# Turning the SSD results on VectorE in 32x32 blocks, with four block-placing transfers per chunk, and the norm weight moved to the feature split

## The chip, the cores and the metric

One core of a Trainium2 chip runs the whole program. The metric is device time in microseconds (us) of one execution. The engines are TensorE (PE, with its weight loads as PEld), VectorE (DVE), ScalarE (ACT), GpSimd (POOL) and SyncE (SP, which here issues most transfers).

## The reference, cut to what matters

A two-layer network over 1024 latent tokens and 256 context tokens, width 1024. Layer 0 is windowed attention; layer 1 is a bidirectional Mamba-2 SSD mixer with 32 heads of 64 in 8 groups, so 256 features in a group, scanned in chunks of 128 tokens. Its last step, `back`, is what the change touches:

```
def back(y_f, y_b, xs, z):
    n = xs.shape[1]
    y = y_f + y_b + d_skip.astype(f32).reshape(SSD_GROUPS, SSD_HEADS_PER_GROUP, 1) * xs
    u = y.reshape(bsz, n, SSD_WIDTH) * jax.nn.silu(z.astype(f32))
    u = rms_normalize(u.reshape(bsz, n, SSD_GROUPS, SSD_WIDTH // SSD_GROUPS))
    return (u.reshape(bsz, n, SSD_WIDTH) * norm_w) @ w_out
```

The norm is taken per token over the 256 features of a group. `norm_w` has one number for each of the 2048 features, and `@ w_out` sums over the features, so TensorE needs the features on partitions for it.

## The kernel before, in words

All float32 products are made of two rounded halves, "high" (fp32r) and "low" (the rest), with three matmuls each (high·high, high·low, low·high). Layer 0 takes the first 800 us or so; the change lies in layer 1, in `ssd` and `ssd_out`.

`ssd` runs 8 groups of 8 chunks: 64 calls of `slot`, one for each chunk of each group. A slot makes, for 128 tokens (partitions) and 256 features (columns):

- `pcb` (L1281), `po` (L1283, L1284) and, but for a group's last chunk, the state update `S` (L1290) on PE, into banks of the PSUM ring psX (three buffers);
- the decay matrix: `load_rows` (L1260) has SP bring the rows `fd` and `bd` from DRAM two chunks ahead, `offset` (L1264) on POOL adds a column to `bd`, `decays` merges them on DVE (L1269) and takes four exponentials on ACT (L1271); L1285 on DVE multiplies by `pcb`;
- the output: eight PE passes (L1310, `yd`, in psX), added to the POOL sum on DVE (L1319), multiplied by the gate (L1320), squared and summed on ACT (L1322), raised to -1/2 on POOL (L1323), and scaled on ACT (L1328). The result stands in one of two buffers `y`.

While a slot runs, `fill` hands PE the projections of the next group (`front`: L1142, L1151, L1176, with transposes L1084, and DVE work L1037, L1045, L1064), or in the last group the output projection (`ssd_out`, L1570). So there are always matmuls to put between the steps of a slot.

The result of a slot has tokens on partitions. Its `tail` is called in the next slot, after that one's L1310. It turns the 128x256 block with two PE transposes (L1340) into a fourth tenant of psX, ACT evicts each half and multiplies it by the norm weight (L1341; after the turn a feature is a partition, so the weight is a column), and SP writes `uT` to the DRAM tensor `uN` in one transfer (L1342), in rows of 128 tokens, 512 bytes.

In `ssd_out`, SP fetches the features back, 128 features by 512 tokens at a time (L1516, `oraw`), and `split` makes their halves: ACT copies the high half (L1528), DVE subtracts it for the low half (L1525). 32 such pieces feed L1570.

Within the program order that the code gives, a scheduler decides from its own cost estimates where each instruction stands on its engine, and inserts the waits. Each engine runs its own list strictly in that order. SP's list matters too: a transfer that waits for its data holds up all transfers behind it. SP's transfers take their completion semaphores from a ring of eight, so one may also wait for the landing of the eighth before it.

Of the kernel before, what the change touches and what calls it, by code (L numbers as in the profile page):

```python
# [9 lines left out]
F32 = mybir.dt.float32  # L10
BF16 = mybir.dt.bfloat16
F32R = mybir.dt.float32r
AF = mybir.ActivationFunctionType
ALU = mybir.AluOpType
# [3 lines left out]
P = 128  # L18
# [85 lines left out]
class Kernel:  # L104
# [13 lines left out]
    def t(self, pool, shape, dt, tag, bufs=None):  # L118
        self.n += 1
        kw = {"bufs": bufs or BUFS.get(tag, 1)}  # L120
        return pool.tile(shape, dt, tag=tag, name=f"{tag}_{self.n}", **kw)
# [1070 lines left out]
    def ssd(self, c0):  # L1192
        nc, t, a = self.nc, self.t, self.a
        ps = self.psA
# [4 lines left out]
        p = self.ps_ = self.pool("sfront", ctx=c0)  # L1199
# [75 lines left out]
        def slot(n, st, M, fill, tick, last):  # L1275

            g, c = divmod(n, NCH)
            cs = slice(c * P, (c + 1) * P)
            xc = X(st, c).rearrange("p (r h) -> p r h", r=R)
            pcb = t(ps, [P, 512], F32, "psX")[:, :P]  # L1280
            nc.tensor.matmul(pcb, st["bT"][:, cs], st["cT"][:, cs], start=True, stop=True)  # L1281
            po = t(ps, [P, 512], F32, "psX")
            nc.tensor.matmul(po[:, :256], st["cT"][:, cs], flat(st["hf"]), start=True, stop=True)  # L1283
            nc.tensor.matmul(po[:, 256:], st["cT"][:, cs], flat(st["hb"][c]), start=True, stop=True)  # L1284
            nc.vector.tensor_tensor(M, M, pcb.unsqueeze(1).broadcast_to([P, R, P]), op=ALU.mult)  # L1285
            if c < NCH - 1:
                S = t(ps, [P, 512], F32, "psX")
                hn = t(ps2, [P, R, HP], F32, "hf")
                decay(hn, st["hf"], g, c, 0)
                nc.tensor.matmul(S[:, :256], B(st, c), flat(st["xw"]), start=True, stop=True)  # L1290
                nc.vector.tensor_add(hn, hn, S[:, :256].rearrange("p (r h) -> p r h", r=R))
                st["hf"] = hn
            y2 = t(ps2, [P, 2, R, HP], F32, "y2")
            nc.vector.tensor_tensor(y2, po.rearrange("p (d r h) -> p d r h", d=2, r=R),
                                    self.eacs[:, c, :].rearrange("p (d q) -> p d q", d=2)[:, :, 4 * g : 4 * g + 4].unsqueeze(3).broadcast_to([P, 2, R, HP]), op=ALU.mult)
            fill(0)
            xs = t(ps2, [P, R, HP], F32, "xs")
            dg = t(ps2, [P, 1], F32, "dg")
            nc.vector.tensor_tensor_reduce(out=flat(xs)[:, :P], in0=pcb, in1=self.ident, scale=1.0, scalar=0.0, op0=ALU.mult, op1=ALU.add, accum_out=dg)
            sk = t(ps2, [P, R], F32, "sk")  # L1300
            nc.vector.scalar_tensor_tensor(sk, in0=self.dtb[:, c, 4 * g : 4 * g + 4], scalar=dg, in1=self.dsk[:, 4 * g : 4 * g + 4], op0=ALU.mult, op1=ALU.add)
            y = ys[n % 2]
            yf = y[:, :256]
            yv = yf.rearrange("p (r h) -> p r h", r=R)
            nc.gpsimd.tensor_tensor(xs, xc, sk.unsqueeze(2).broadcast_to([P, R, HP]), op=ALU.mult)
            nc.gpsimd.tensor_tensor(yv, y2[:, 0], y2[:, 1], op=ALU.add)
            yadd = nc.gpsimd.tensor_tensor(yv, yv, xs, op=ALU.add)
            yd = t(ps, [P, 512], F32, "psX")
            for r in range(R):
                nc.tensor.matmul(yd[:, r * HP : (r + 1) * HP], M[:, r], X(st, c)[:, r * HP : (r + 1) * HP], start=True, stop=True)  # L1310
            if self.tail is not None:
                self.tail(t(ps, [P, 512], F32, "psX"))
            fill(1)
            load_rows(n + 2, 0)
            nM = None
            if n + 1 < G * NCH:
                with self.tc.issue_after(yadd.ins):
                    offset(n + 1)
            nc.vector.tensor_add(yv, yv, yd[:, :256].rearrange("p (r h) -> p r h", r=R))  # L1319
            ymul = nc.vector.tensor_mul(yf, yf, st["sz"][c])  # L1320
            ss = t(ps2, [P, 1], F32, "ss", 2)
            nc.scalar.activation(y2.rearrange("p d r h -> p (d r h)")[:, :257], y[:, :257], AF.Square, scale=1.0 / 16.0, accum_out=ss)  # L1322
            nc.gpsimd.tensor_tensor(ss, ss, self.half, op=ALU.pow)  # L1323
            fill(2)
            if n + 1 < G * NCH:
                with self.tc.issue_after(ymul.ins):
                    nM = decays(n + 1)
            nc.scalar.activation(yf, yf, AF.Copy, scale=ss)  # L1328
            if c < NCH - 2:
                st["xw"] = xweight(st, g, c + 1, 0)  # L1330
            tick()
            fill(3)
            tick()
            fill(4)
            tick()

            def tail(pt):
                uT = t(ps2, [P, 2, P], F32, "uT")
                for e in range(2):
                    nc.tensor.transpose(pt[:, e * P : (e + 1) * P], yf[:, e * P : (e + 1) * P], self.ident)  # L1340
                    nc.scalar.activation(uT[:, e], pt[:, e * P : (e + 1) * P], AF.Copy, scale=self.nw[:, 2 * g + e : 2 * g + e + 1])  # L1341
                nc.sync.dma_start(self.uN_d[g][:, :, cs].rearrange("e p n -> p e n"), uT)  # L1342

            self.tail = tail
            return nM
# [42 lines left out]
        with ExitStack():  # L1388
            for g in range(G):
                nst = {}  # L1390
                if g < G - 1:
                    work, total = self.front(g + 1, nst, post, st.get("next")), FRONT
                else:
                    cf.close()
                    post.flush()
                    work, total = self.ssd_out(self.pool("out", ctx=c0, side="right"), [(p, [P, 2, 512], F32, "xn4")] * 4, p, ps2, post), OUT * 0.85
                spent = 0.0
                chain = None

                def run(until):  # L1400
                    nonlocal spent
                    while spent < until:
                        cost = next(work, None)
                        if cost is None:
                            return
                        spent += cost
                        post.run(cost)

                def tick():
                    nonlocal chain  # L1410
                    if g < G - 1 and 1 in nst:
                        chain = chain or states(g + 1, nst)
                        next(chain, None)

                for c in range(NCH):
                    def fill(x):
                        run(total * (c + sum(SEGS[: x + 1]) / sum(SEGS)) / NCH)
                    M = slot(g * NCH + c, st, M, fill, tick, g == G - 1)
                if g < G - 1:
                    run(1e9)  # L1420
                    while 1 not in nst or not nst["sz"]:
                        post.pop()
                    chain = chain or states(g + 1, nst)
                    for _ in chain:
                        pass
                    nst["xw"] = xweight(nst, g + 1, 0, 0)
                    st = nst
            self.tail(t(ps, [P, 512], F32, "psX"))
        for _ in work:
            pass  # L1430

    def ssd_out(self, p, spare, sp, sc, post):
# [39 lines left out]
        def tail(s, n, h, r, k, m0):  # L1472
            for m in range(m0, m0 + k):
                if m % 2:
                    nc.gpsimd.tensor_tensor(h[m], h[m], r, op=ALU.mult)
                    nc.scalar.activation(h[m], h[m], AF.Copy, scale=fw[:, m : m + 1])
                else:
                    nc.vector.scalar_tensor_tensor(h[m], in0=h[m], scalar=fw[:, m : m + 1], in1=r, op0=ALU.mult, op1=ALU.mult)
            src = h[m0] if k == 1 else pair[m0][:, :, s - 512 : s - 512 + n]
            dst = a["out"][m0 * P : (m0 + k) * P, s : s + n]  # L1480
            nc.sync.dma_start(dst if k == 1 else dst.rearrange("(a p) n -> p a n", p=P), src)
# [36 lines left out]
        def split():  # L1518
            n = put[0]
            if n < len(feats):  # L1520
                put[0] += 1
                hi, lo = dst[order[n]]

                def low():
                    nc.vector.tensor_sub(lo, feats[n], hi)  # L1525
                    ready.add(order[n])

                post.extend([lambda: nc.scalar.copy(hi, feats[n]), low])  # L1528

        self.oH, self.oL = [None] * 2, [None] * 2  # L1530
        for e in range(2):
# [217 lines left out]
```

## Time and profile before

| | |
|---|---|
| three timed runs | 1806.45, 1807.05, 1812.54 us (median 1807.05) |
| profiled execution | 1804.25 us |
| its span, first to last instruction | 1802.2 us |
| SSD chunks, from the first to the last PE transpose of `tail` | 872 to 1694 us of the span |
| PE busy in that stretch | 817.17 of 822 us |
| DVE, ACT, POOL busy in it | 562.29, 362.94, 409.11 us |
| granted clock of TensorE | 0.994 mean, 1.00 in that stretch |

A profile row such as `L1340 PE MATMUL psX<-ident,y 128*128 128x128 f32 x128 | 35.1, 274 | 0.0` names the line, the engine, the operation, the output and inputs by the program's names, shapes and count; then busy microseconds in all, mean nanoseconds of one, and the idle time of the engine just before these instructions. A timeline row starts with the start and the duration in us. PE instructions overlap: one may start before the one ahead of it has ended, so what a matmul takes of PE's time is the distance from start to start, not its duration.

### The profile page before, as it was taken

The page shows a single profiled execution, that of the slowest core. Times are in us where ns is not written, and L with a number is a line of the kernel's source. Part 1 is how long each engine was busy: PE and PEld are TensorE (multiplying, and loading weights), DVE is VectorE, ACT ScalarE, POOL GpSimd, SP SyncE. Part 2 cuts the span into 40 slices and gives each one's busy share as a digit, 9 for nine tenths or more (in the row PEclk, how much of TensorE's full clock was granted, in tenths as well). Part 3 has the DMA queues.
Part 4 walks back from the last instruction along what each step waited for, and adds up shares of the span by engine and source line. Part 5 has one row for each costly group of instructions (what it writes and reads, how often), then busy time and mean ns, then how long its engine had stood idle before and what let it go on. Part 6 is the DMA issues. An engine that isn't in the chain of part 4 may idle for free.

```text
span 1802.2 us, 28825 instructions
## 1 busy us (share of the span) xinstructions
PE 1741.2 (97%) x10243; PEld 1488.7 (83%) x10243; DVE 1162.7 (65%) x2110; ACT 875.4 (49%) x1897; POOL 815.5 (45%) x1070
## 2 busy tenths in 40 slices
PE   6999998999999899999999999999999999999997
PEld 4797767788898787778898898989889898988886
DVE  3564537787777766675766848667584866765743
ACT  3522235777788666352443534434352443544532
POOL 2441127654466465303454554645455464554422
PEclk9999999999999999999999999999999999999998
DMA  8758865543345445311322323233232333555533
GB/s 300 288 155 256 264 187 149 126 112 96 97 127 131 115 135 196 108 40 51 86 73 79 94 61 92 80 77 82 76 96 62 92 78 80 175 153 174 188 101 123
DMA packets 209391, 227.87 MB, mean 126 GB/s; under 512 B 16096, under 2 KB 149088, under 8 KB 208224
## 3 DMA queue, kind: packets, MB, share of 16 engines
q1 hardware_dynamic: 175184, 207.38, 37.7%
q0 software_dynamic: 34064, 18.65, 5.7%
q8 instruction: 81, 1.33, 0.3%
q14 instruction: 62, 0.51, 0.1%
HBM read 191.14 MB, written 35.13 MB: 126 GB/s over the span
## 4 chain that ended last, share of the span: by engine, by line
PE 85%; DVE 6%; ACT 4%; DMA 3%; issue 2%; SPq 0%; POOL 0%; DVEq 0%; ACTq 0%; POOLq 0%
PE pj L1151 17%; PE pj L1176 10%; PE pj L1570 7%; PE pj L222 7%; PE pj L224 6%; PE pj L223 6%; PE psD L1142 3%; PE pt L693 3%; PE psX L1310 2%; PE pv L700 2%; PE psD L1235 2%; PE pv L699 2%; PE S L668 2%; PE psX L1284 1%; PE psX L1283 1%
## 5 line engine op out<-in xcount | busy, mean ns | idle before, releaser
L222 PE MATMUL pj<-uH,wh 128*128 128x512 f32 (+1 forms) x604 | 223.2, 370 | 6.7 <-DVE rope_b L531 2.3
L224 PE MATMUL pj<-uH,wl 128*128 128x512 f32 (+1 forms) x604 | 211.3, 350 | 0.0
L223 PE MATMUL pj<-uL,wh 128*128 128x512 f32 (+1 forms) x604 | 210.3, 348 | 0.0
L210 POOL TENSOR_TENSOR wl<-wr,wh 128x512 fp32r<-128x512 f32 x92 | 121.7, 1326 | 97.8 <-ACT wh L208 96.6
L1151 PE MATMUL pj<-uH,wh 128*128 128x512 f32 x480 | 161.2, 410 | 2.0 <-ACT xn L1087 1.2
L1151 PE MATMUL pj<-uH,wl 128*128 128x512 f32 x480 | 158.5, 403 | 0.0
L1151 PE MATMUL pj<-uL,wh 128*128 128x512 f32 x480 | 157.2, 401 | 0.0
L698 DVE TENSOR_TENSOR pl<-pt,ph 128x512 fp32r<-128x512 f32 x168 | 114.3, 688 | 60.9 <-ACT ph L697 60.1
L1176 PE MATMUL pj<-wh,uH 128*128 128x256 f32 x512 | 148.0, 289 | 3.1 <-ACT xn L1087 3.0
L1176 PE MATMUL pj<-wl,uH 128*128 128x256 f32 x512 | 150.7, 294 | 0.0
L1212 POOL TENSOR_TENSOR xw<-xn,dtdec 128x256 f32<-128x256 f32 x144 | 93.2, 651 | 127.0 <-PE psD L1235 108.6
L1176 PE MATMUL pj<-wh,uL 128*128 128x256 f32 x512 | 149.5, 292 | 0.0
L222 PEld LDWEIGHTS pj<-uH,wh 128*128 128x128 f32 x604 | 114.2, 189 | 35.2 <-issue 7.8
L1341 ACT ACTIVATE uT<-psX,nw 128x128 f32<-128x128 f32 x128 | 46.9, 366 | 192.9 <-PE psX L1340 192.7
L672 DVE CUSTOM_DVE_ANT_0 sm<-S,mask,nsink 128x640 f32<-128x640 f32 (+2 forms) x160 | 118.8, 773 | 23.2 <-PE S L669 11.5
L208 ACT CAST wh<-wr 128x512 fp32r<-128x512 f32 (+1 forms) x132 | 84.9, 646 | 92.9 <-PE pj L223 73.2
L224 PEld LDWEIGHTS pj<-uH,wl 128*128 128x128 f32 x604 | 114.0, 189 | 17.2 <-issue 1.9
L697 ACT CAST ph<-pt 128x512 fp32r<-128x512 f32 x168 | 97.6, 586 | 62.1 <-PE pt L693 56.3
L223 PEld LDWEIGHTS pj<-uL,wh 128*128 128x128 f32 x604 | 114.5, 190 | 13.1 <-issue 2.5
L674 ACT ACTIVATE sm<-sm,nm 128x640 f32<-128x640 f32 (+2 forms) x160 | 118.6, 742 | 12.2 <-DVE nm L672 11.9
L1151 PEld LDWEIGHTS pj<-uL,wh 128*128 128x128 f32 x480 | 90.1, 188 | 18.9
L1151 PEld LDWEIGHTS pj<-uH,wh 128*128 128x128 f32 x480 | 89.1, 188 | 19.6 <-ACT bn L1087 2.0
(390 smaller groups left out, 5004.6 us busy)
## 6 DMA issues: line engine op xcount, KB each, us to landing
fd<-acs SPq DMA_DIRECT2D x64, 256.0 KB, 5.0
bd<-acs SPq DMA_DIRECT2D x64, 256.0 KB, 5.3
wr<-w_x SPq DMA_DIRECT2D x31, 512.0 KB, 4.0
wr<-w_sk SPq DMA_DIRECT2D x24, 512.0 KB, 4.2
wr<-wg SPq DMA_DIRECT2D x44, 256.0 KB, 4.7
qs<-q POOLq DMA_DIRECT2D x40, 256.0 KB, 3.8
wr<-wo SPq DMA_DIRECT2D x40, 256.0 KB, 2.6
wada<-w_ad SPq DMA_DIRECT2D x8, 1024.0 KB, 6.5
```

Source lines behind the costliest of these rows:

```text
L210: (eng or nc.vector).tensor_tensor(l, raw, h, op=ALU.subtract)
L222: self.nc.tensor.matmul(ps, lh, rh, start=first and i == 0, stop=False)
L223: self.nc.tensor.matmul(ps, lh, rl, start=False, stop=False)
L224: self.nc.tensor.matmul(ps, ll, rh, start=False, stop=last and i == n - 1)
L672: nc.vector.tensor_tensor_reduce(out=sm[:, :W], in0=Sv, in1=self.mask[:, m0 : m0 + W], scale=-SCALE, scalar=self.nsink[:, 4 * j + r : 4 * ...
L674: nc.scalar.activation(sm[:, :W], sm[:, :W], AF.Exp, bias=nm[:, r : r + 1], scale=-1.0, accum_out=sums[:, r : r + 1])
L697: nc.scalar.copy(ph, ptf)
L698: nc.vector.tensor_sub(pl, ptf, ph)
L1151: nc.tensor.matmul(raw[:, 512 * i : 512 * i + 512], l[:, k, :], r[i][:, k, :], start=k + y == 0, stop=k == KT - 1 and y == 2)
L1176: nc.tensor.matmul(pj[:, c], l, r[:, k, :], start=c % 2 + q + k + y == 0, stop=c % 2 == 1 and q == 1 and k == 3 and y == 2)
L1212: nc.gpsimd.tensor_tensor(xw, X(st, c).rearrange("p (r h) -> p r h", r=R), self.dtdec[:, c, hd(d, g)].unsqueeze(2).broadcast_to([P, R, HP] ...
L1570: nc.tensor.matmul(banks[x], l[:, z, sl], r, start=k == 2 * qs[0] and y == 0, stop=k == 2 * qs[-1] + 1 and y == 2)
```

## The change

The tail no longer uses PE, ACT and PSUM. One VectorE instruction turns the 128x256 block in 32x32 squares: token 32b+j, feature 32f+i goes to partition 32b+i, column 32f+j. Each band of 32 partitions then holds 32 tokens of all 256 features, and one transfer for each band puts its blocks where they belong in `uN`: 256 pieces of 32 tokens, 128 bytes each. So a chunk takes four transfers in place of one, and 1024 pieces in place of 256. Since a feature is no longer alone on a partition in `uT`, the norm weight is left out there; `split` applies it, as a column scale in the ACT copy and in the DVE subtraction.

```
-                self.tail(t(ps, [P, 512], F32, "psX"))
+                self.tail()
...
-            def tail(pt):
-                uT = t(ps2, [P, 2, P], F32, "uT")
-                for e in range(2):
-                    nc.tensor.transpose(pt[:, e * P : (e + 1) * P], yf[:, e * P : (e + 1) * P], self.ident)
-                    nc.scalar.activation(uT[:, e], pt[:, e * P : (e + 1) * P], AF.Copy, scale=self.nw[:, 2 * g + e : 2 * g + e + 1])
-                nc.sync.dma_start(self.uN_d[g][:, :, cs].rearrange("e p n -> p e n"), uT)
+            def tail():
+                uT = t(ps2, [P, 256], F32, "uT")
+                nc.vector.transpose(uT, yf)
+                for b in range(4):
+                    dst = self.uN_d[g].rearrange("e (b p) n -> p (e b) n", p=32)[:, :, c * P + 32 * b : c * P + 32 * b + 32]
+                    nc.sync.dma_start(dst, uT[32 * b : 32 * b + 32].rearrange("p (f n) -> p f n", n=32))
...
                 hi, lo = dst[order[n]]
+                nw = self.nw[:, order[n][1] : order[n][1] + 1]
 
                 def low():
-                    nc.vector.tensor_sub(lo, feats[n], hi)
+                    nc.vector.scalar_tensor_tensor(lo, in0=feats[n], scalar=nw, in1=hi, op0=ALU.mult, op1=ALU.subtract)
                     ready.add(order[n])
 
-                post.extend([lambda: nc.scalar.copy(hi, feats[n]), low])
+                post.extend([lambda: nc.scalar.activation(hi, feats[n], AF.Copy, scale=nw), low])
```

The scheduler places the changed program anew from the first tail on. Both places below are from the fourth chunk of the sixth group and the chunk after it. The first is PE's list before: from one chunk's L1310 to the next chunk's `po` and state update (psX_15442 is the ring buffer that the transposes fill; cacc, cctx, pj and psD belong to the projections).

```order
L1310 MATMUL psX_15437<-xn_3030_13955,fd_15206 128x64
L1084 MATMUL psD_15220<-ident_63,cctx_15262 128x128 x2
L1310 MATMUL psX_15437<-xn_3030_13955,fd_15206 128x64 x3
L1340 MATMUL psX_15442<-ident_63,y_2198_9138 128x128
L1281 MATMUL psX_15532<-cT_14508,bT_14012 128x128
...
L1340 MATMUL psX_15442<-ident_63,y_2198_9138 128x128
...
L1283 MATMUL psX_15534<-hf_15411,cT_14508 128x256
L1284 MATMUL psX_15534<-hb_3188_14866,cT_14508 128x256
L1290 MATMUL psX_15538<-xw_15505,bn_3034_13959 128x256
```

PE's list in the changed program at the same place.

```order
L1310 MATMUL psX_15395<-xn_2999_13924,fd_15165 128x64 x4
L1281 MATMUL psX_15489<-cT_14472,bT_13980 128x128
L1283 MATMUL psX_15491<-hf_15369,cT_14472 128x256
L1284 MATMUL psX_15491<-hb_3150_14828,cT_14472 128x256
L1084 MATMUL pj_3253_15413<-ident_63,cacc_15414 128x128 x2
...
L1290 MATMUL psX_15495<-xw_15462,bn_3003_13928 128x256
...
L1310 MATMUL psX_15516<-xn_3000_13925,fd_15305 128x64 x4
```

The two transposes are gone, and with psX no longer shared by the tail, the next chunk's `pcb` and `po` stand directly behind L1310. Left out in the changed list, between this L1310 and the next, are 24 matmuls of L1142, 5 of L1151 and 6 transposes of L1084.

The second place is VectorE's list before, from this chunk's L1285 to the next chunk's.

```order
L1285 TENSOR_TENSOR fd_15206<-fd_15206,psX_15404 128x512
L1299 ISA xs_15429,dg_15430<-psX_15404,ident_63 128x128
...
L1294 TENSOR_TENSOR y_3288_15415<-psX_15406,eacs_8749 128x512
L1291 TENSOR_TENSOR hf_15411<-hf_15411,psX_15410 128x256
L1319 TENSOR_TENSOR y_2199_9140<-y_2199_9140,psX_15437 128x256
L1320 TENSOR_TENSOR y_2199_9140<-y_2199_9140,sz_14840 128x256
L1269 COPY_PREDICATED fd_15347<-before_8755,bd_15240 128x512
L1285 TENSOR_TENSOR fd_15347<-fd_15347,psX_15532 128x512
```

VectorE's list in the changed program at the same place.

```order
L1285 TENSOR_TENSOR fd_15165<-fd_15165,psX_15362 128x512
L1299 ISA xs_15387,dg_15388<-psX_15362,ident_63 128x128
...
L1339 STREAM_TRANSPOSE uT_15400<-y_2198_9138 128x256
L1045 SCALAR_TENSOR_TENSOR cacc_15414<-pj_3253_15413,cacc_15414 128x1024
...
L1319 TENSOR_TENSOR y_2199_9140<-y_2199_9140,psX_15395 128x256
L1320 TENSOR_TENSOR y_2199_9140<-y_2199_9140,sz_14802 128x256
L1269 COPY_PREDICATED fd_15305<-before_8755,bd_15199 128x512
L1294 TENSOR_TENSOR y_3265_15500<-psX_15491,eacs_8749 128x512
L1285 TENSOR_TENSOR fd_15305<-fd_15305,psX_15489 128x512
```

The turn L1339 (of the chunk before) stands behind L1285 and L1299, ahead of projection work and of this chunk's L1319; L1294 has moved from ahead of L1319 to behind L1269. On SP's list the four `uN` transfers stand in a row where one stood, and the next chunk's row load `fd` behind them.

More of the change, by code (lines that the diff above doesn't have):

```diff
@@ L1427, in ssd @@
                     st = nst
-            self.tail(t(ps, [P, 512], F32, "psX"))
+            self.tail()
         for _ in work:
```

## The prediction

> **What bounds the kernel now.** I read the page first, then the busy time by stage, then what PE waited for in the stage of the change. The page says that PE is the fullest engine.
>
> ```profile
> PE 1741.2 (97%) x10243; PEld 1488.7 (83%) x10243; DVE 1162.7 (65%) x2110; ACT 875.4 (49%) x1897; POOL 815.5 (45%) x1070
> ```
>
> An average says little about one stage, so here are the busy times of the stretch that holds all chunks, and of what follows (columns: stretch, length, busy us and instructions of PE, PEld, DVE, ACT, POOL, granted clock, DMA share, GB/s).
>
> ```profile
> 872.00:1694.00 822.00, 817.17 (x4948) 725.38 (x4947) 562.29 (x956) 362.94 (x831) 409.11 (x556) 1.00 0.36 99
> ...
> 1694.00:1802.00 108.00, 98.92 (x485) 82.48 (x483) 50.90 (x54) 40.63 (x61) 29.93 (x19) 0.96 0.37 118
> ```
>
> PE is busy for all but 4.8 us of the 822. Its waits there (total us, times, longest) are small, and none is for the tail's work.
>
> ```profile
> PE pj L1176 <- ACT xn L1087: 2.1, 6, 0.3
> PE pj L1084 <- ACT xn L1087: 1.6, 6, 0.3
> PE pj L1570 <- DVE sz L1187: 0.2, 1, 0.2
> ```
>
> So the chunks are bound by how many passes PE is given, not by the chunk's own chain: what is taken from PE's list comes off the end, and work put on VectorE is free until it makes PE wait. Both have to be priced.
>
> **The change part by part.** *The PE transposes go.* Their busy row is not their price, since passes overlap. The price is the distance of starts, in a timeline of PE around one of them.
>
> ```profile
> 897.98 0.61 PE L1151 MATMUL pj<-uH,wh 128*128 128x512 f32 x2
> 898.43 0.39 PE L1151 MATMUL pj<-uL,wh 128*128 128x512 f32 x1
> 898.66 0.27 PE L1340 MATMUL psX<-ident,y 128*128 128x128 f32 x1
> 898.69 0.48 PE L1151 MATMUL pj<-uL,wh 128*128 128x512 f32 x1
> 899.01 0.63 PE L1151 MATMUL pj<-uH,wl 128*128 128x512 f32 x2
> 899.48 0.62 PE L1151 MATMUL pj<-uH,wh 128*128 128x512 f32 x2
> ```
>
> Two 512-column passes take 0.45 to 0.47 us from start to start. From 898.43 to 899.01, 0.58 us, there are two of them and one transpose, which so costs 0.11 to 0.13 us; I take 0.11. All groups of the tail, before:
>
> ```profile
> L1341 ACT ACTIVATE uT<-psX,nw 128x128 f32<-128x128 f32 x128 | 46.9, 366 | 192.9 <-PE psX L1340 192.7
> ...
> L1340 PE MATMUL psX<-ident,y 128*128 128x128 f32 x128 | 35.1, 274 | 0.0
> ```
>
> 128 x 0.11 = 14.1 us leave PE. ACT loses 46.9 us, which is worth nothing by itself: ACT was busy for 363 of 822 us.
>
> The Trainium skill prices a PE transpose higher ("TensorE: Matmul & The Clock Gate", Part 4: PE-mode transpose): about 275 ns for 128x128 in one kernel's context. The trace agrees with that as a duration, 274 ns, and not as what the pass costs among others, 0.11 us.
>
> *The turn comes to VectorE.* No row shows it. The nearest is the shuffle across partitions, on 512 columns; the rows of L1294 (512 columns) and L1319 (256) in the table below say what half the columns do to a duration.
>
> ```profile
> L531 DVE STREAM_SHUFFLE rope_b<-pj 128x512 f32<-128x512 f32 x20 | 14.8, 739 | 0.0
> ```
>
> 739 x 417 / 687 = 0.45 us, my value. From below it is bounded by an add of that size, 0.42, and from above by the longest VectorE row in these chunks, 1.31 (L1064). 64 x 0.45 = 29 us, so VectorE goes from 562 to 591 us, 72% of the stretch: cover on average, but not everywhere. The new order packs the chunks more tightly. The costliest VectorE groups from 1100 to 1560 us (columns as on the page):
>
> ```profile
> L1064 DVE TENSOR_TENSOR wl<-wr,wh 128x1024 fp32r<-128x1024 f32 x26 | 34.0, 1306 | 15.4 <-ACT wh L1060 15.4
> L1269 DVE COPY_PREDICATED fd<-before,bd 128x512 f32<-128x512 int32 x36 | 32.0, 889 | 0.0
> L1037 DVE SCALAR_TENSOR_TENSOR cacc<-pj,cw,cacc 128x1022 f32<-128x1022 f32 x19 | 24.3, 1278 | 4.5 <-ACT cacc L1033 4.5
> L1294 DVE TENSOR_TENSOR y<-psX,eacs 128x512 f32<-128x512 f32 x35 | 24.1, 687 | 21.1 <-PE psX L1284 20.5
> L1285 DVE TENSOR_TENSOR fd<-fd,psX 128x512 f32<-128x512 f32 x35 | 23.9, 683 | 10.9 <-ACT fd L1271 7.5 <-PE psX L1281 2.9
> L1037 DVE SCALAR_TENSOR_TENSOR cacc<-pj,cw,cacc 128x1023 f32<-128x1023 f32 x18 | 23.0, 1276 | 0.2
> L1320 DVE TENSOR_TENSOR y<-y,sz 128x256 f32<-128x256 f32 x36 | 19.0, 528 | 0.7
> L1319 DVE TENSOR_TENSOR y<-y,psX 128x256 f32<-128x256 f32 x36 | 15.0, 417 | 26.2 <-PE psX L1310 19.5 <-POOL y L1307 6.7
> ```
>
> Count the changed order over four intervals from the second to the sixth chunk of a group. VectorE has there four each of L1285, L1294, L1269, L1320 and L1319 (4 x 3.20 = 12.8 us), 7 wide L1037 and one wide L1045 at 1.28 (10.2), 3 L1064 (3.9) and 22 short rows, which I put at L1319's 0.42 (9.2): 36.1 us, and 3 turns, 37.5 in all. PE has 61 passes of 512 columns at 0.23 us (14.0), 122 of 256 at half of that (14.0) and, at the transpose's pace of 0.11 us for 128 columns, 9.2 us of float32 work (12 transposes L1084; two passes each for 4 L1281 and, with 256 columns, for 12 of L1283, L1284 and L1290; 32 passes of 64 columns, L1310): 37.2 us. The two are even. If VectorE falls behind, L1285 comes late, L1310 waits for it, and PE stands, since its list is fixed. What cushion there is shows in the old timeline, in the tightest chunk of a group:
>
> ```profile
> 1201.50 0.68 DVE L1285 TENSOR_TENSOR fd<-fd,psX 128x512 f32<-128x512 f32 x1
> ...
> 1202.66 1.00 PE L1310 MATMUL psX<-xn,fd 128*128 128x64 f32 x8
> ```
>
> L1285 ends at 1202.18, and L1310 starts 0.48 us later. An excess of 0.3 us is inside that cushion, but the count leaves out the hand-overs between engines; so I give back 0.2 us in each of 7 groups, 1.5 us in all (from 0 to the price in the second rival).
>
> *One transfer becomes four.* SP pays three more issues; the transfer rows below give 0.36 us each, 1.1 us for a chunk. The first of the four waits for VectorE's turn, and behind it are queued the row load `fd` and weight loads. Who would wait for them is L1269. Its tightest case before:
>
> ```profile
> 1547.19 0.39 SPq L1260 DMA_DIRECT2D fd<-acs  x1
> ...
> 1558.27 1.16 DVE L1269 COPY_PREDICATED fd<-before,bd 128x512 f32<-128x512 int32 x1
> ```
>
> From issue to use are 11.1 us. The rows for landing of those loads (min, median, max), for the `uN` issues (first three numbers, ns), and for the queues (packets, MB, share of 16 engines' time):
>
> ```profile
> DMA to landing us min/median/max: 4.4/5.2/8.4
> L1342 SPq DMA_DIRECT2D uN<-uT x64: 359/360/783, 877.9 to 1694.5; - x64
> q1 hardware_dynamic: 175184, 207.38, 37.7%
> q0 software_dynamic: 34064, 18.65, 5.7%
> ```
>
> So 5.9 us are spare at the median landing. A packet took 0.377 x 16 x 1802.2 / 175184 = 62 ns of one engine at 1184 bytes on the one queue, and 48 ns at 547 bytes on the other. Packets of 128 bytes no row shows: by bytes alone they would take 7 ns, and 62 is the upper bound of these rows; I take 40, near the smaller one. A chunk then puts 1024 x 40 / 16 = 2.6 us on the engines where it put 256 x 48 / 16 = 0.8; at 62, 4.0. With the issues, loads come 1.1 + 1.8 = 2.9 us later, at worst 4.3. Both are under 5.9, so I cost it at nothing; without that cover every chunk would pay the excess.
>
> A rule of the Trainium skill speaks against this part ("DMA: Bandwidth & Descriptors", Specifications): transfers below 512 bytes fall under line rate, because the engine does read-modify-write. No run here shows it; a third rival takes it up.
>
> *The norm weight.* ACT's plain copy becomes a scaled one, and DVE's subtraction takes a scalar. The two as they are now, a scaled ACT copy of that size from the kernel's end, a VectorE operation with a scalar, and the last stretch of L1570 in the chain that ended last:
>
> ```profile
> L1528 ACT CAST uH<-oraw x32: 609/622/627, 1572.8 to 1711.0; 128x512 fp32r<-128x512 f32 x32
> L1525 DVE TENSOR_TENSOR uL<-oraw,uH x32: 673/686/1783, 1573.5 to 1711.7; 128x512 fp32r<-128x512 f32 x32
> L1595 ACT ACTIVATE xn<-xn,fw x7: 710/715/727, 1745.1 to 1779.5; 128x512 f32<-128x512 f32 x7
> L1576 DVE SCALAR_TENSOR_TENSOR xn<-pj,mod,xn x4: 741/746/751, 1742.3 to 1744.4; 128x512 f32<-128x512 f32 x4
> 1733.54 8.79 PE pj L1570 x38
> ```
>
> 32 x 0.09 = 3.0 us on ACT and 32 x 0.06 = 1.9 us on DVE. The last piece is split at 1712, and PE works on L1570 until 1742; its final 24 passes, which need that piece, take 5.5 us. So 24 us of other matmuls cover the last `uN` transfers, the fetch behind them and the split. Uncovered, it would be 5 us.
>
> *The sum.* 1804.25 (profiled; the span is 1802.2) - 14.1 + 1.5 = 1791.6, a gain of 12.6 us. The median of the three runs lies 2.8 us above the profiled time, so I predict 1807.05 - 12.6 = 1794.4.
>
> **The rivals.** *PE gives more.* The idle 4.8 us of the stretch could also go, as ACT is freer for the evictions L1087 that PE waited for, and psX has one tenant less: gain 14.1 + 4.8 = 18.9, 1788. For it: the PE waits are on ACT. Against: the order is tighter, not looser. Chance 0.06. If every transpose were worth its whole duration, the gain would be 35.1 us, 1772; the start distances contradict it: 0.02. The page's 275 ns would make the same of it.
>
> *VectorE becomes the bound.* If the turn takes 1.31 us in place of 0.45, VectorE exceeds PE by 0.3 + 3 x 0.86 = 2.9 us in the four intervals; less the 0.48 of cushion that is 2.4 us in each of 7 groups, 17 us: the gain is gone, 1807 - 14 + 17 = 1810. At a turn of 1.0 us the excess is 1.5 us and 10 us are lost, 1803. For it: the even count. Against: VectorE's mean of 72%, and long intervals elsewhere in a group that refill the cushion. Chance 0.17.
>
> *The transfers make it slower.* If a 128-byte packet takes twice the 62 ns, a chunk's transfers occupy 7.9 us, 7.1 more than now, and loads come 8.2 us later: 2.3 us over the spare 5.9. Stalls of that size in a quarter of the 64 chunks, and of 1 us in half of the others, make 16 x 2.3 + 24 x 1.0 = 61 us, so 1807 - 14 + 61 = 1854. It decides from 5.9 us of lateness, some 90 ns a packet. For it: four waits in SP's list and small pieces. Against: a DMA share of only 0.36 in this stretch. By the skill's rule above this is the case to fear. Chance 0.07.
>
> That the change does not do what it says is excluded: PE's list has lost its 128 rows of L1340.
>
> **How the numbers follow.** Forecast 0.68, more gain 0.08, VectorE 0.17, transfers 0.07. A difference of 0.5% (9 us) is about what a measurement of this kernel can tell from no change. Faster by more than that: the forecast but for its worst tenth, 0.61, more gain, 0.08, and a mild VectorE loss, 0.02: 0.71. Within it: 0.07 + 0.15 = 0.22. Slower: 0.07. The forecast by itself spans 1790 to 1799. The range takes half of the first rival and most of the second: 1789 to 1806, leaving out some 0.15.
>
> **What would show it.** Right: no L1340, a stretch of chunks some 13 us shorter, PE still over 99% busy in it, L1339 at about 0.45 us, DVE busy some 590 us, `fd` loads landing within 8 us, nothing waiting for them. Wrong: PE waits at L1310 for `fd` from L1285 (VectorE), or L1269 waiting for DMA (transfers); packets of `uN` far above 40 ns.

## The result

The changed kernel is slower, not faster: 1822.06 us in the median of five runs (1819.15 to 1824.04), against 1807.05 us for the kernel before in its five. The ratio of the two is 1.0070 with a 95% interval of 1.0049 to 1.0091, so some 13 us are lost (0.7%; the two medians lie 15.0 us apart) where 12.6 us of gain were forecast. The profiled execution took 1819.45 us, its span 1817.7.

### The profile page after: what moved, and what is told of

It reads as the page before. It is cut to its first block, busy times and chain, and to the rows that moved or that the text cites. A ratio compares the mean times of both kernels' runs of the same rounds, so it can differ in the third digit from the quotient of the medians.

```text
span 1817.7 us, 28697 instructions
## 1 busy us (share of the span) xinstructions
PE 1740.4 (96%) x10115; PEld 1486.6 (82%) x10115; DVE 1189.4 (65%) x2174; ACT 841.4 (46%) x1769; POOL 809.2 (45%) x1070
## 4 chain that ended last, share of the span: by engine, by line
PE 81%; DVE 6%; DMA 5%; ACT 4%; issue 2%; POOL 1%; SPq 0%; DVEq 0%; ACTq 0%; POOLq 0%
PE pj L1151 17%; PE pj L1176 9%; PE pj L222 6%; PE pj L224 6%; PE pj L223 6%; PE pj L1571 6%; PE psD L1142 3%; PE pt L693 3%; PE psX L1310 2%; PE pv L700 2%; PE pv L699 2%; PE psD L1235 2%; PE S L668 2%; PE S L669 1%; PE psX L1284 1%
## 5 line engine op out<-in xcount | busy, mean ns | idle before, releaser
L1212 POOL TENSOR_TENSOR xw<-xn,dtdec 128x256 f32<-128x256 f32 x144 | 100.0, 699 | 183.9 <-PE psD L1235 144.9
L1151 PE MATMUL pj<-uH,wh 128*128 128x512 f32 x480 | 158.3, 405 | 4.8 <-ACT xn L1087 4.5
L1151 PE MATMUL pj<-uH,wl 128*128 128x512 f32 x480 | 156.0, 402 | 1.2 <-DVE wl L1064 1.2
L1151 PE MATMUL pj<-uL,wh 128*128 128x512 f32 x480 | 156.8, 402 | 0.0
L224 PEld LDWEIGHTS pj<-uH,wl 128*128 128x128 f32 x604 | 114.0, 189 | 17.2 <-issue 1.9
L1151 PEld LDWEIGHTS pj<-uH,wh 128*128 128x128 f32 x480 | 90.0, 189 | 23.7 <-ACT xn L1087 5.2
L1151 PEld LDWEIGHTS pj<-uH,wl 128*128 128x128 f32 x480 | 90.6, 190 | 21.4 <-DVE wl L1064 2.8
L1151 PEld LDWEIGHTS pj<-uL,wh 128*128 128x128 f32 x480 | 90.6, 190 | 18.7
```

What stands on the lines that cost most here:

```text
L224: self.nc.tensor.matmul(ps, ll, rh, start=False, stop=last and i == n - 1)
L1151: nc.tensor.matmul(raw[:, 512 * i : 512 * i + 512], l[:, k, :], r[i][:, k, :], start=k + y == 0, stop=k == KT - 1 and y == 2)
L1212: nc.gpsimd.tensor_tensor(xw, X(st, c).rearrange("p (r h) -> p r h", r=R), self.dtdec[:, c, hd(d, g)].unsqueeze(2).broadcast_to([P, R, HP] ...
```

## The profile after

The page's PE line of the changed kernel. PE does 128 passes less and is busy for as long as before (1741.2 us).

```profile
PE 1740.4 (96%) x10115; PEld 1486.6 (82%) x10115; DVE 1189.4 (65%) x2174; ACT 841.4 (46%) x1769; POOL 809.2 (45%) x1070
```

Busy times by stretch, from the first chunks to the last of L1570 (L1571 now), first of the kernel before, then of the changed one (columns as in the prediction):

```profile
872.00:1742.00 870.00, 865.17 (x5163) 765.11 (x5162) 585.38 (x978) 381.77 (x857) 420.26 (x563) 1.00 0.36 100
```
```profile
872.00:1757.00 885.00, 863.26 (x5053) 762.00 (x5052) 612.72 (x1045) 350.38 (x731) 419.07 (x567) 0.99 0.39 99
```

PE stands still for 4.8 us of the one stretch and for 21.7 us of the other: the change made PE wait 16.9 us more. What it waits for, in the changed kernel, in the same stretch (total us, times, longest):

```profile
PE psD L1235 <- DVE hb L1247: 5.0, 5, 2.3
PE pj L1151 <- ACT xn L1087: 3.3, 2, 2.6
PE psX L1284 <- DVE hb L1247: 2.6, 3, 0.9
PE pj L1176 <- ACT xn L1087: 2.6, 1, 2.6
PE psD L1235 <- ACT hx L1239: 1.8, 1, 1.8
PE pj L1571 <- ACT xn L1466: 1.7, 1, 1.7
```

The rows with `hb` and `hx` come to 9.4 us, and none of them belongs to the tail that was edited. They are of the state steps: during a group's chunks, a side chain (`states`) works out the entry states of the next group. One step is a PE product (L1235) into the single `psD` buffer, an add on VectorE (L1247), which empties that buffer, and the decay of the result on GpSimd (L1217), which the next step's add needs. Here is that chain at the end of a group, in the timeline of the changed kernel, the other rows left out.

```profile
1404.54 0.60 PE L1235 MATMUL psD<-xw,bn 128*128 128x256 f32 x2
...
1405.24 0.42 DVE L1247 TENSOR_TENSOR hb<-hb,psD 128x256 f32<-128x256 f32 x1 [1.61 <-PE psD L1235]
...
1405.72 0.70 PE L1235 MATMUL psD<-xw,bn 128*128 128x256 f32 x2 [0.58 <-DVE hb L1247]
1405.79 0.62 POOL L1217 TENSOR_TENSOR hb<-hb,eal 128x256 f32<-128x256 f32 x1
...
1406.78 0.41 DVE L1247 TENSOR_TENSOR hb<-hb,psD 128x256 f32<-128x256 f32 x1
...
1408.54 0.65 PE L1235 MATMUL psD<-xw,bn 128*128 128x256 f32 x2
...
1409.82 0.41 DVE L1247 TENSOR_TENSOR hb<-hb,psD 128x256 f32<-128x256 f32 x1
...
1410.28 0.70 PE L1284 MATMUL psX<-hb,cT 128*128 128x256 f32 x2 [0.87 <-DVE hb L1247]
```

One step takes 1.54 us from add to add, and PE's list asks for them faster, so PE stands: 0.58 us here, 0.87 us where the next group's first chunk (L1284) needs the state. In the kernel before, the last steps of the same group come 4.8 and 5.5 us apart, the last of them ahead of the next group's first L1310, and PE waits for none (its timeline, other rows left out):

```profile
1380.52 0.59 PE L1235 MATMUL psD<-xw,bn 128*128 128x256 f32 x2
...
1385.99 0.59 PE L1235 MATMUL psD<-xw,bn 128*128 128x256 f32 x2
...
1386.86 1.00 PE L1310 MATMUL psX<-xn,fd 128*128 128x64 f32 x8
...
1390.75 0.59 PE L1284 MATMUL psX<-hb,cT 128*128 128x256 f32 x2
```

The state steps are not the whole of the waits. The two longest, 2.6 us each, lie in the third group (they end at 1114.2 and 1138.4 us), where no L1235 runs between 1077 and 1147 us. There PE waits for an eviction, L1087, of what its transposes L1084 left in `pj` by 1111.6 us. On ACT's list that eviction stands behind the chunk's exponentials (L1271) and its scaling (L1328):

```profile
1110.94 1.20 ACT L1033 ACTIVATE cacc<-pj,cb,cw 128x1024 f32<-128x1024 f32 x1
1112.03 1.27 ACT L1271 ACTIVATE fd<-fd,vf 128x128 f32<-128x128 f32 x4
1113.20 0.50 ACT L1328 ACTIVATE y<-y,ss 128x256 f32<-128x256 f32 x1
1113.60 0.57 ACT L1087 COPY xn<-pj 128x512 f32<-128x512 f32 x1
```

The waits cost more than their length. The stretches of 10 us of the changed kernel in which the granted clock (the third number from the end) is below 1.00; before the change there is none from 872 to 1742 us:

```profile
1110.00:1120.00 10.00, 7.36 (x28) 5.73 (x27) 9.90 (x19) 4.51 (x12) 4.74 (x7) 0.83 0.57 115
1130.00:1140.00 10.00, 7.41 (x43) 6.40 (x42) 9.45 (x18) 6.83 (x14) 3.43 (x4) 0.93 0.46 132
1140.00:1150.00 10.00, 10.00 (x75) 9.84 (x75) 9.14 (x16) 3.91 (x10) 6.36 (x10) 0.90 0.35 88
1580.00:1590.00 10.00, 8.24 (x53) 7.96 (x53) 6.38 (x10) 6.53 (x10) 3.19 (x4) 0.83 0.70 203
1600.00:1610.00 10.00, 6.38 (x20) 4.22 (x19) 8.36 (x16) 4.35 (x10) 7.73 (x10) 0.83 0.69 185
```

The missing clock adds up to 1.7 + 0.7 + 1.0 + 1.7 + 1.7 = 6.8 us. Each place lies on or right behind one of four long waits: 2.6 and 2.6 us for L1087, 1.8 and 2.3 us for state steps. A wait of 1.7 us, the last row above, has no such place behind it.

The pieces that the prediction priced, in the changed kernel: the turn, the transfers' issues and landing, the landing of the row loads, the queue, and the split with the norm weight.

```profile
L1339 DVE STREAM_TRANSPOSE uT<-y x64: 424/440/448, 870.3 to 1715.1; 128x256 f32<-128x256 f32 x64
L1342 SPq DMA_DIRECT2D uN<-uT x256: 303/442/1900, 870.7 to 1716.9; - x128
DMA to landing us min/median/max: 4.5/5.3/8.6
q1 hardware_dynamic: 227408, 207.40, 39.2%
L1529 ACT ACTIVATE uH<-oraw,nw x32: 707/722/727, 1581.2 to 1727.0; 128x512 fp32r<-128x512 f32 x32
L1526 DVE SCALAR_TENSOR_TENSOR uL<-oraw,nw,uH x32: 728/750/1785, 1582.0 to 1727.8; 128x512 fp32r<-128x512 f32 x32
```

They are what was said, nearly: 0.44 us a turn, row loads that land as before (at most 8.6 us), split operations of 0.72 and 0.75 us.

## The theories

**Order theory**: the pieces cost what the prediction said, and the loss comes from where the new lists put other work, the state steps above all. **VectorE theory**: the turn's 28 us on VectorE themselves make PE wait. **Transfer theory**: the small pieces and SP's four waits delay what stands behind them.

The order theory can be read in the lists. Weighing each PE pass with its pace (0.23 us for 512 columns), I counted pairs of neighbouring state steps less than 1.9 us apart, from the second group on: 2 in the kernel before and 12 in the changed one; at the worst places no other PE work stands between two steps, as at 1404.54 and 1405.72 us above.

## The experiments

For each run, the ratio with its interval, taken to runs of the kernel before beside it (whose medians lie between 1807.05 and 1810.33 us), and in the profiled execution the stretch from the first pass of L1310 to the start of the last pass of L1570 or its like. That stretch leaves out the stages ahead of the chunks, whose end wandered from 857 to 868 us among kernels whose work there is the same (876 in before_states_late).

| kernel | median us | ratio (95%) | stretch us | close pairs |
|---|---|---|---|---|
| before | 1807.05 | 1 | 886.4 | 2 |
| changed | 1822.06 | 1.0070 (1.0049 to 1.0091) | 897.6 | 12 |
| four_transfers | 1807.38 | 1.0002 (0.9990 to 1.0015) | 886.5 | 2 |
| turn_added | 1809.94 | 1.0005 (0.9994 to 1.0017) | 887.6 | 2 |
| three_turns | 1808.90 | 0.9996 (0.9982 to 1.0009) | 886.0 | 2 |
| norm_at_split | 1810.91 | 1.0015 (1.0002 to 1.0029) | 887.7 | 2 |
| no_turn | 1790.98 | 0.9901 (0.9886 to 0.9916) | 866.5 | 2 |
| one_transfer | 1822.62 | 1.0074 (1.0055 to 1.0094) | 898.5 | 12 |
| states_first | 1798.54 | 0.9941 (0.9925 to 0.9957) | 873.6 | 4 |
| states_raised_10 | 1798.99 | 0.9943 (0.9926 to 0.9960) | 874.8 | 2 |
| before_states_first | 1804.24 | 0.9971 (0.9958 to 0.9984) | 881.7 | 0 |
| before_raised_10 | 1810.42 | 1.0010 (0.9994 to 1.0026) | 886.3 | 2 |
| before_states_late | 1847.47 | 1.0216 (1.0194 to 1.0239) | 909.1 | 11 |

**The transfers alone** (four_transfers), on the kernel before:

```diff
-                nc.sync.dma_start(self.uN_d[g][:, :, cs].rearrange("e p n -> p e n"), uT)
+                for b in range(4):
+                    dst = self.uN_d[g][:, :, c * P + 32 * b : c * P + 32 * b + 32].rearrange("e p n -> p e n")
+                    nc.sync.dma_start(dst, uT[:, :, 32 * b : 32 * b + 32])
```

> The kernel before, with only its uN transfer cut into four of 32 columns each: 128-byte pieces, 16,384 more bytes-sized pieces of work per queue than before, PE transposes kept. The instruction lists of PE, VectorE and ScalarE are those of before up to the last group. Order theory (the loss of the change comes from where the new lists put the state steps L1235; the pieces themselves cost what the prediction said): 1807 us, within 4. Transfer theory (small pieces and four waits delay the row loads): 1817 to 1825 us. VectorE theory (the turn's own time makes PE wait): 1807 us.

The time is that of before, with an interval of 0.15% to either side; the transfer theory falls. The 16,384 pieces of 512 bytes became 65,536 of 128 bytes (49,152 more, not the 16,384 of the text above), and the queue shows it:

```profile
q1 hardware_dynamic: 227408, 207.40, 39.8%
```

Its time is 0.398 x 16 x 1806.9 = 11,506 us of one engine, before 0.377 x 16 x 1802.2 = 10,871. If each piece that went took 48 ns (the prediction's figure, the mean of another queue) they took 786 us before, so the new ones take (635 + 786) / 65,536 = 0.022 us: an estimate of 22 ns, not 40. For a quarter of the bytes that is about half the time, so the rate of such a piece falls by nearly half. The rule of the Trainium skill on transfers below 512 bytes ("DMA: Bandwidth & Descriptors", Specifications) agrees with that in kind; whether a read-modify-write is behind it no run here shows. The kernel lost no time by it, with a DMA share of 0.36 in the stretch before.

**The changed kernel with one transfer** (one_transfer):

```diff
-                for b in range(4):
-                    dst = ...
-                    nc.sync.dma_start(dst, uT[32 * b : 32 * b + 32].rearrange("p (f n) -> p f n", n=32))
+                nc.sync.dma_start(self.uN_d[g][:, :, cs].rearrange("e p n -> p e n"), uT.rearrange("p (e n) -> p e n", e=2))
```

> The changed kernel with one transfer per chunk in place of four, in 512-byte pieces as before, so that the blocks stay where the turn left them and only the times are read. The lists of PE have the same close pairs of state steps. Order theory: as slow as the changed kernel, 1817 to 1824 us. Transfer theory: 1793 to 1800 us.

As slow as the changed kernel, with its 12 close pairs: taking the small pieces away gives nothing back.

**VectorE's turn alone** (turn_added; three_turns has the new line three times):

```diff
                 uT = t(ps2, [P, 2, P], F32, "uT")
+                nc.vector.transpose(uT.rearrange("p e n -> p (e n)"), yf)
```

> The kernel before, with a VectorE turn of y added in each chunk (its result is overwritten by the PE transposes' copies), so VectorE gets the 28 us and PE loses nothing. The state steps stay at least 2.5 us apart in PE's list from the second group on. VectorE theory: PE waits 15 us or more, 1821 to 1830 us. Order theory: 1807 to 1811 us. Transfer theory: 1807 us.

> The kernel before with three turns of y in VectorE's list per chunk, all overwritten by the PE transposes' copies: 84 us more of VectorE, which is then fuller than in the changed kernel, while the state steps stay 2.4 us or more apart in the later groups. Order theory: 1808 to 1815 us, well under the changed kernel. VectorE theory: 1825 us or more.

Neither moves the time. Here are three_turns' turns, and its stretch:

```profile
L1339 DVE STREAM_TRANSPOSE uT<-y x192: 418/439/448, 876.9 to 1706.7; 128x256 f32<-128x256 f32 x192
```
```profile
872.00:1754.00 882.00, 878.49 (x5226) 777.08 (x5225) 659.40 (x1187) 392.54 (x869) 426.72 (x572) 1.00 0.36 100
```

VectorE is busy for 659 of 882 us, 47 us more than in the changed kernel's 885, and PE stands for 3.5 us. The VectorE theory falls: PE can be fed with VectorE at 75% in this order.

**The changed kernel without the turn** (no_turn):

```diff
-                uT = t(ps2, [P, 256], F32, "uT")
-                nc.vector.transpose(uT, yf)
+                uT = yf
```

> The changed kernel without the turn: the four transfers of 128-byte pieces send y as it stands, so the normalised results are stored in the wrong places and only the times are read. The state steps stand at least 2.5 us apart again. Order theory and VectorE theory: 1791 to 1798 us, the 14 us of the transposes gained. Transfer theory: about 1820 us.

It is 0.99% faster, 17.9 us by the median of before in that comparison, 1808.66. So the gain from PE's list exists and is a little more than forecast. In the kernel before, the same chunk's L1310 comes 105.50 us later in each group (1300.00 and 1405.50); without the turn it is 102.45 us:

```profile
1296.03 1.00 PE L1310 MATMUL psX<-xn,fd 128*128 128x64 f32 x8
...
1398.48 1.00 PE L1310 MATMUL psX<-xn,fd 128*128 128x64 f32 x8
```

Of the 3.05 us, 0.6 are the waits for L1087 that went too; 2.45 / 16 = 0.15 us is what a PE transpose cost. In three_turns, which keeps them and waits for nothing in these groups, a group takes 104.4 us, and the same sum gives 0.12.

**The state steps moved in the list** (states_first; states_raised_10 has 10 for 200). The work is that of the changed kernel, the turn and the four transfers included.

```diff
-                s = t(ps, [P, 512], F32, "psD")[:, :256]
-                nc.tensor.matmul(s, B(st, c), flat(xw.pop(n)), start=True, stop=True)
+                with self.tc.high_priority(offset=200):
+                    s = t(ps, [P, 512], F32, "psD")[:, :256]; nc.tensor.matmul(s, B(st, c), flat(xw.pop(n)), start=True, stop=True)
...
```

(The rest of the step stands inside the same block.)

> The changed kernel, with the state steps (L1235, their decay and add) raised in the scheduler's priority by 200: all work kept, turn and four transfers too; in PE's list no two state steps stand closer than 0.67 us, where the changed kernel has twelve pairs within 0.23 to 1.8 us from the third group on. Order theory: 1792 to 1800 us, hardly any PE wait for hb L1247 left. VectorE theory: 1815 us or more, the waits move to other rows. Transfer theory: about 1820 us.

> The changed kernel with the state steps raised by 10 in place of 200: from the second group on all state steps but one or two stand 2.5 us or more apart in PE's list, as in the kernel before, and nothing else is pushed behind them by more than this. Order theory: PE's 14 us come out whole, and the 6.9 us that PE waited for ScalarE's L1087 in states_first should shrink too: 1789 to 1796 us. If those waits belong to the turn itself: 1797 to 1801 us. VectorE theory: 1815 us or more.

Both are 0.6% faster than before and so (0.994 / 1.007) 1.3% faster than the changed kernel, by the list alone. PE's waits in states_first, from 872 to 1742 us:

```profile
PE pj L1151 <- ACT xn L1087: 4.3, 3, 1.4
PE pj L1176 <- ACT xn L1087: 2.7, 4, 0.7
PE psD L1235 <- DVE hb L1247: 1.4, 1, 1.4
```

The waits for `hb` and `hx` fell from 9.4 to 1.4 us, and in this stretch no 10 us have a clock below 1.00. The two waits of 2.6 us for L1087 went too, though none of the raised steps stood near them: raising the steps moved the rest of the lists as well. Shorter waits for ScalarE's L1087 stay in this one; in states_raised_10 they shrink to 1.4 us, but others come (2.2 us for `hf` L1291, 1.2 for `xw` L1212, with 1.7 us of clock lost behind one of 1.6 us), and the time is the same, not the 1789 to 1796 us that I expected of it. The steady groups of states_raised_10 take 102.86 us, near no_turn's 102.45:

```profile
1285.04 1.00 PE L1310 MATMUL psX<-xn,fd 128*128 128x64 f32 x8
...
1387.90 1.00 PE L1310 MATMUL psX<-xn,fd 128*128 128x64 f32 x8
```

It lacks 8.3 us of the stretch against no_turn. PE's waits (6.0 against 2.5 us) and the 1.7 us of clock are 5.2 of them; where the rest lies is not shown, since outside the steady groups the two lists spread the projections differently.

**Controls on the kernel before** (before_states_first, before_raised_10, before_states_late: the same block with 200, 10 and -100):

> The kernel before with its state steps raised in priority by 200, the control for states_first. Order theory: PE waited only 4.8 us in these 822 us, so there is little to gain: 1802 to 1809 us. If raising the steps were a gain by itself, apart from the change: 1797 us, 10 us under before.

> The kernel before with the state steps raised by 10, the control: its list was spaced already. Order theory: 1804 to 1809 us.

> The kernel before with nothing changed in its work, only its state steps (L1235, decay, add) lowered in the scheduler's priority by 100: PE's list then holds eleven pairs of state steps within 1.9 us of each other from the third group on, as the changed kernel's does. Order theory: slower than before by as much as such waits cost in the changed kernel, 8 to 20 us, 1815 to 1828 us, with PE waiting for hb L1247. VectorE theory (no turn here): 1807 us, within 4.

Raised by 10, the list was spaced already, and nothing moves. So at equal priority, 10 in both, the change is worth 886.3 - 874.8 = 11.5 us of the stretch, and 0.67% of the time by the two ratios: near the 12.6 us that were forecast. Raised by 200, the kernel before gains 0.29%, so part of states_first's gain is the list's and not the change's: there the change is worth 881.7 - 873.6 = 8.1 us of the stretch, and 0.30% by the ratios. Lowered by 100, a kernel with no turn and its one transfer loses 2.2%, which is more than the change lost and more than I expected. Of the profiled 43 us some 19 lie ahead of the first chunk (its first L1310 starts at 876.1 us against 856.9), and 22.7 in the stretch, from which 65 PE passes have moved ahead of the first chunk. Yet its longest rows of waits there are not all of the state steps (the transposes' buffers and the split at the end wait as well):

```profile
PE psD L1235 <- DVE hb L1247: 2.8, 2, 2.2
PE pj L1570 <- DVE uL L1576: 2.8, 1, 2.8
PE psX L1283 <- ACT uT L1341: 2.7, 6, 0.5
```

So this run shows that the place of these steps alone can cost tens of microseconds; it does not show that their own waits are the whole of it, since moving them moves the rest.

**The norm weight alone** (norm_at_split), the diff's part in the split, and L1341 without its scale:

> The kernel before with the norm weight moved to the split alone: PE transposes, their copies (now without the weight) and the one transfer kept. All theories: 1807 us, within 4; if the scaled split were on the path at the end, up to 1812 us.

1.0015 (1.0002 to 1.0029), 2.7 us, with 1.3 us more in the stretch: within what was expected, and at the edge of what can be told from nothing.

## Why the prediction was wrong

**What bounds the kernel** was right: PE's list. no_turn took passes from it, and the end came earlier by their price.

**The transposes' price** was right in kind and a little small: 0.12 to 0.15 us each, 15 to 19 us, where I had 0.11 and 14.1.

**The turn's price** was right: 0.44 us against 0.45, and its rival, VectorE as the bound by its sheer time, is refuted by three_turns and, with the change's own work, by states_first. The count that made VectorE and PE even was off, to the other side: the same four intervals of the sixth group (1423.86 to 1464.03 us in the changed kernel) take 40.17 us, where I had 37.2 of PE, and VectorE is busy for 33.6 of them with four turns, where I had 37.5 with three.

**The transfers at nothing** was right: four_transfers. The pieces took some 22 ns, by the estimate above, where I took 40. The issues took more, 0.44 us where I had 0.36, and the row loads still landed in time.

**The norm weight at nothing** was right within 3 us.

**The step that failed** is in the second term: "so I give back 0.2 us in each of 7 groups, 1.5 us in all". In its place stand 16.9 us more of waits and 6.8 us of lost clock. I had seen that the new order was tighter, and then checked one chain at one place, L1285 to L1310 in the middle of a group, with a count of VectorE's work against PE's. Neither place that I named for being wrong, L1310 or L1269, shows in PE's waits above. The largest part of the waits, 9.4 us with 3.4 us of the lost clock, came from a chain that the change does not touch, which the new list had pushed to the end of the group, its last steps close together around the chunk that needs the last of them. The next, 5.2 us with the other 3.4 of clock, came from the eviction L1087 on ACT's list, which my first rival expected to wait less. The chain's part could have been seen before the run: count the state steps that stand closer in the new list than the 1.5 us that a step takes. For L1087 no such count is shown.

The balance of the stretch, 897.6 - 886.4 = 11.2 us: the transposes give -15 to -19, the waits +16.9, the clock +6.8, which is 5 to 9 us. The rest, 2 to 6 us, fits the steady groups: from 1407.70 to 1513.34 us the changed kernel takes 105.64 us, and without its 2.2 us of waits still 1.0 more than no_turn. Part of it is the pass ahead of a wait, which has no other behind it to overlap with. In the changed kernel's stretch 24 passes stand so and hold PE for 8.0 us in all, where passes of the same lines elsewhere take 3.5 us from start to start; no_turn has 4 of them, 1.6 us against 0.8. What is left is not accounted for. The remaining 4 us between the two profiled times lie ahead of the chunks (first L1310 at 861.2 against 856.9). four_transfers, which is no slower than before, has 861.5 there, so they are put down to the execution and not to the change.

What stays open is why the scheduler put the steps late. Fewer PE passes alone (no_turn) didn't do it, nor did one or three turns alone (turn_added, three_turns); the two together did, with four transfers or with one.

## What to carry to other kernels

Where a scheduler sets the order, an edit is priced twice: by the instructions that it adds and takes, and by the list that comes out. Read the new list for every chain that PE waits on, not only the edited one, and compare the distance of a chain's steps in PE's list with the time that one step takes; where it was shorter here, PE stood. Look at the evictions on the other engines' lists too: here they made the two longest waits. If a change that should gain loses, move the chain in the list before giving up the change: here one line of priority turned 0.7% lost into 0.6% gained.

## What the hardware showed

Waits of 1.8 to 2.6 us were followed by a lower clock. Behind the one of 2.64 us, in the changed kernel's PE timeline, two 512-column passes take 0.85 us from start to start for some 4 us, and then 0.46 again:

```profile
1114.22 0.87 PE L1151 MATMUL pj<-uH,wh 128*128 128x512 f32 x2 [2.64 <-ACT xn L1087]
1114.89 1.05 PE L1151 MATMUL pj<-uL,wh 128*128 128x512 f32 x2
...
1118.20 0.63 PE L1151 MATMUL pj<-uH,wl 128*128 128x512 f32 x2
1118.66 0.62 PE L1151 MATMUL pj<-uH,wh 128*128 128x512 f32 x2
```

The Trainium skill ("TensorE: Matmul & The Clock Gate", Part 1) puts the loss of clock behind an idle window of about 3.4 us; halved clock and the length of the slow spell agree, but shorter waits came ahead of it here: 1.8 us in the changed kernel, 1.6 us in states_raised_10. Their length alone doesn't decide it: the wait of 1.7 us in the changed kernel and three of 1.4 us in states_first had no slow spell behind them. And VectorE took 192 turns in three_turns, against 64 in the changed kernel, and lost no time against the kernel before: a busy share, even of 75%, says little about who waits.
